# One full norm for two token tiles ahead of a 16-bit matrix product, in a two-layer decoder trunk

## The chip, the cores and the metric

The kernel runs on one NeuronCore of a Trainium2 chip. The metric is the time of one execution in device microseconds (us). Comparisons use the median of several runs. Engines are named as in the profile: PE is TensorE (matmuls; PEld its weight loads), DVE is VectorE, ACT is ScalarE, POOL is GpSimd, SP issues most of the transfers.

## What is computed

A trunk of two layers over 512 tokens of width 1024. Layer 0 has an attention mixer with two head groups (MoBA and NSA), layer 1 a forgetting attention (FoX). Each mixer is followed by a squared-ReLU MLP, and it is the two MLPs that the change touches. Cut to that part:

```python
def rmsnorm(x, g):
    xf = x.astype(jnp.float32)
    y = xf * lax.rsqrt(jnp.mean(xf * xf, axis=-1, keepdims=True) + RMS_EPS)
    return (y * g.astype(jnp.float32)).astype(x.dtype)

def sqrelu_mlp(h, w1, w2):
    a = jax.nn.relu(h @ w1)
    return (a * a) @ w2
...
for layer in range(DEPTH):
    hn = rmsnorm(h, mix_norm[layer])
    if layer % 2 == 0:
        h = h + moba_nsa_mixer(hn, ...)
    else:
        h = h + fox_mixer(hn, ...)
    h = h + sqrelu_mlp(rmsnorm(h, mlp_norm[layer]), mlp_w1[layer], mlp_w2[layer])
return rmsnorm(h, final_norm)
```

The hidden width of the MLP is 4096.

## The kernel before, in words

**Tiling.** The 512 tokens lie in four tiles of 128 (`hs[0]` to `hs[3]`, 128 partitions by 1024 columns). Matrix products get their accuracy from pairs: each operand is split into a high and a low part, and three matmuls (high by high, high by low, low by high; lines 135 to 137 in `mm3`) make one product.

**Banks.** PSUM has eight banks of 128 x 512 fp32 words. The program names them in four pairs, by tag: `s` (attention logits, later MLP results), `acc` (projections), `o` (attention outputs) and `pt` (transposes). `self.psum(tag)` takes a bank of the pair; it is free again when its last reader is through.

**Order of the work.** The program is written down in the order of `MIX0_ORDER` and `FOX_ORDER`, strings of steps. A planner then lays the instructions of every engine in a fixed order, by priorities and by a simulated timeline; so a change in one place can reorder work in another. In `MIX0_ORDER` the last steps are `m3 y o17 o6 o23`: the last pair of MoBA heads, step `y` (`prepare_rest`), and then three out-projections (`out_proj`, line 678 adds each result to `hs`) over head pairs 1 and 7, 6, and 2 and 3. In `FOX_ORDER` they are `p7 y o45 o67`. An out-projection runs over four token tiles and two halves of the columns, so eight bank-sized results, with three matmuls for each head pair in it. Its O tiles (the attention outputs, split in high and low) live in a pool of three buffers in layer 0.

**Step y.** The weights of the first MLP product are scaled into a 16-bit range by powers worked out from sums of squares. `scales16` adds up the sums over the partitions by a matmul with a matrix of ones (line 421), copies the result out of its bank (line 426) and makes the scale and its inverse on DVE (lines 427 to 429). In step `y` this is called with the tag `acc`; the matmul is tied to run behind `pv_last`, the last matmul of the attention so far, and the copy behind `v_last`, the last DVE step of the attention (in layer 0 the head sum of line 655). `up_split` then makes the 16-bit high and low weights (line 447 on ACT, 448 on DVE).

**The norm.** `norm_t16` handles the token tiles one by one. ACT squares the tile and sums it (line 388), DVE makes from this sum a rough factor `near` by bit operations on the number (lines 391 to 393), scales the tile by it and by the norm's weights in two halves (line 395), PE transposes eight blocks (line 400), ACT makes the 16-bit high part (line 403) and DVE the low part (line 404). As `near` is only near the true factor, a correction for each token is worked out afterwards (`row()`: full inverse root by `newton`, over `near`). `spread_row` turns it into a row along the free axis: four POOL products with the identity (line 195), a matmul with ones (line 196), a copy (line 197).

**The MLP.** It runs in eight steps of 512 hidden columns. `up(s)` makes four products of 128 hidden columns over all tokens; the product of `up(0)` is split in two halves of the tokens and held in four banks (two `acc`, two `s`). For every product ACT takes the relu and undoes the weights' scale (line 1189), POOL multiplies by the row (line 1190), and ACT squares (line 1192). `down(s)` multiplies with the second weight matrix by a Strassen scheme: `combos` makes sums of the activations (POOL, lines 1210 to 1215; splits on ACT, line 1200, and DVE, line 501), `weights` sums of the weights (line 1249 on DVE; splits on lines 1243 and 1244), PE runs line 1292, and DVE adds to `hs` (line 1300). The order of calls is `up(s + 1)` ahead of `down(s)`; the scales for `up(s + 2)` are made within `down(s)`.

Of the kernel before, what the change touches and what calls it, by code (L numbers as in the profile page):

```python
# [7 lines left out]
F32 = mybir.dt.float32  # L8
FR = mybir.dt.float32r
I32 = mybir.dt.int32  # L10
F16 = mybir.dt.float16
AF = mybir.ActivationFunctionType
ALU = mybir.AluOpType
AX = mybir.AxisListType

P = 128
S = 512
D = 1024
NT = S // P
# [5 lines left out]
RMS_EPS = 1e-5  # L25
ROOT_BITS = 0x5F3759DF
# [8 lines left out]
W_RAW = 1024  # L35
# [15 lines left out]
class Trunk:  # L51
# [133 lines left out]
            v.tensor_tensor(u, u, m, op=ALU.mult)  # L185
            v.scalar_tensor_tensor(y, u, -1.5, y, op0=ALU.add, op1=ALU.mult)

    def spread_row(self, y, sq_pool, pool):

        nc = self.nc  # L190
        diag = sq_pool.tile([P, S], F32, tag="r", name=self.nm("diag"))
        row = pool.tile([P, S], F32, name=self.nm("yrow"))
        ps = self.psum("pt")
        for t in range(NT):
            nc.gpsimd.tensor_scalar(diag[:, t * P:(t + 1) * P], self.ident, y[:, t:t + 1], 1.0, op0=ALU.mult, op1=ALU.mult)
        nc.tensor.matmul(ps, self.ones, diag, start=True, stop=True)
        nc.scalar.activation(row, ps, AF.Copy)
        return row

    def norm(self, h, dst, g):  # L200

        y = self.inv_rms(h, (0, D), lambda i: dst)
        for c in (slice(0, D // 2), slice(D // 2, D)):
            self.nc.vector.scalar_tensor_tensor(dst[:, c], h[:, c], y, g[:, c], op0=ALU.mult, op1=ALU.mult)
# [166 lines left out]
        self.bcast_row(g, row)  # L371
        return g

    def norm_t16(self, hs, g, gain, scratch, sq_pool, pool):

        nc = self.nc
        v = nc.vector
        x = self.xtp.tile([P, 2, KD, S], F16, tag="xhi", name=self.nm("x16"))  # L380
        ssq = pool.tile([P, NT + 1], F32, name=self.nm("ssq"))
        near, m, y, u = (pool.tile([P, NT], F32, name=self.nm("nr")) for _ in range(4))
        for t in range(NT):
            xn = self.raw.tile([P, W_RAW], F32, tag="raw", name=self.nm("xn"))
            one = lambda a: a[:, t:t + 1]
            halves = (slice(0, D // 2), slice(D // 2, D))
            for i, c in enumerate((slice(0, D),) if t < NT - 1 else halves):
                nc.scalar.activation(scratch[:, c], hs[t][:, c], AF.Square, accum_out=ssq[:, t + i:t + i + 1])
            if t == NT - 1:
                v.tensor_tensor(one(ssq), one(ssq), ssq[:, NT:], op=ALU.add)  # L390
            v.tensor_scalar(one(u).bitcast(I32), one(ssq).bitcast(I32), 1, None, op0=ALU.logical_shift_right)
            v.tensor_scalar(one(u).bitcast(I32), one(u).bitcast(I32), -1, ROOT_BITS, op0=ALU.mult, op1=ALU.add)
            v.tensor_tensor(one(near), one(u), gain, op=ALU.mult)
            for c in halves:
                v.scalar_tensor_tensor(xn[:, c], hs[t][:, c], one(near), g[:, c], op0=ALU.mult, op1=ALU.mult)
            for j in range(2):
                pt = self.psum("pt")
                for i in range(4):
                    k = 4 * j + i
                    nc.tensor.transpose(pt[:, i * P:(i + 1) * P], xn[:, k * P:(k + 1) * P], self.ident)  # L400
                pv = pt.rearrange("p (k c) -> p k c", k=4)
                dh, dl = (x[:, i, 4 * j:4 * j + 4, t * P:(t + 1) * P] for i in range(2))
                self.x_act = nc.scalar.activation(dh, pv, AF.Copy)
                self.x_dve = v.tensor_tensor(dl, pv, dh, op=ALU.subtract)  # L404

        def row():
            v.tensor_scalar(m, ssq[:, :NT], 0.5 / D, 0.5 * RMS_EPS, op0=ALU.mult, op1=ALU.add)
            self.newton(m, y, u)
            v.reciprocal(near, near)
            v.tensor_tensor(y, y, near, op=ALU.mult)  # L410
            return self.spread_row(y, sq_pool, pool)
        return (x[:, 0], x[:, 1]), row

    def scales16(self, squares, out, tag, behind=None):

# [42 lines left out]
    def prepare_mlp(self, layer):  # L458

        nc = self.nc  # L460
        st = self.const.tile([P, 3, 5], F32, name=self.nm("upst"))
        g8 = self.const.tile([P, KD], F32, name=self.nm("g8"))
        nc.sync.dma_start(g8, self.I["mlp_norm"][layer].rearrange("(p k) -> p k", k=KD))
        tiles = self.up_tiles(0)
        raws = self.up_load(layer, 0, self.raw, "raw", lambda f: tiles[f][:, 1], st[:, 0])
        nc.scalar.activation(g8, g8, AF.Square, accum_out=st[:, 0, 4:5])

        def rest():
            self.scales16(st[:, 0], st[:, 1:], "acc", self.pv_last)(self.v_last)
            self.first_up = self.up_split(raws, st[:, 1:], tiles), st[:, 1:]  # L470
        self.prepare_rest = rest

# [658 lines left out]
    def mlp(self, layer, hs, final=None):  # L1131
# [4 lines left out]
        nc, I = self.nc, self.I  # L1136
        w1, w2 = I["mlp_w1"][layer], I["mlp_w2"][layer]
        with ExitStack() as cx:
            pool = lambda name, bufs: cx.enter_context(self.tc.tile_pool(name=f"{name}{layer}", bufs=bufs))
            m3 = pool("mlpr", 3)  # L1140
            ma = pool("mlpa", 3)
            mt = pool("mlpt", 1)
            mg = pool("mlpg", 1)
# [5 lines left out]
            scratch = mg.tile([P, W_RAW], F16, name=self.nm("scratch"))  # L1149
            up_sq = [mg.tile([P, 4], F32, name=self.nm("upsq")) for _ in range(2)]  # L1150
            ready = {0: self.first_up}
            load = lambda s, pool, tag, *behind: self.up_load(layer, s, pool, tag, lambda f: scratch, up_sq[s % 2], *behind)

            def up_scale(s, tag, behind=None):
                sc = mg.tile([P, 2, 4], F32, name=self.nm("upsc"))
                return sc, self.scales16(up_sq[s % 2], sc, tag, behind)

            x, norm_row = self.norm_t16(hs, self.row_tile(I["mlp_norm"][layer], "g"), ready[0][1][:, 0, 4:5], scratch, m3, mg)
            after = self.x_act, self.x_dve
            raws1 = load(1, mr, "w", self.x_act)  # L1160
            row = norm_row()
            gf = None
            if final is not None:
                gf = mg.tile([P, D], F32, name="gf")
# [2 lines left out]
            def up(s):  # L1167

                act = [ma.tile([P, 2, 2, S // 2], F32, tag="act", name=self.nm("act")) for _ in range(2)]
                early = {}  # L1170
                w, undo = ready.pop(s)
                if s == 0:
                    tags = ("acc", "acc", "s", "s")
                    early = {f: self.psum(tags[f]) for f in range(nf)}
                    for part in ((0, 256), (256, 512)):
                        for f in range(nf):
                            self.proj_t(early[f], w[f], 0, x, part=part)
                            if part[0] and f == 0:
                                sc, step = up_scale(1, "o", self.mm_last)
                                step(self.x_dve)  # L1180
                                ready[1] = self.up_split(raws1, sc, self.up_tiles(1)), sc
                for f in range(4):
                    if f in early:
                        ps = early[f]
                    else:
                        ps = self.psum("acc")
                        self.proj_t(ps, w[f], 0, x)
                    r = m3.tile([P, S], F32, tag="r", name=self.nm("r"))
                    nc.scalar.activation(r, ps, AF.Relu, scale=undo[:, 1, f:f + 1])  # L1189
                    nc.gpsimd.tensor_tensor(r, r, row, op=ALU.mult)  # L1190
                    rv = r.rearrange("p (l c) -> p l c", l=2)
                    done = nc.scalar.activation(act[f // 2][:, :, f % 2], rv, AF.Square)  # L1192
                    if f == 1:
                        self.up_act = done
                return act
# [129 lines left out]
            def down_plain(s, act):  # L1325
# [3 lines left out]
                for t in range(NT):  # L1329
# [218 lines left out]
```

## Time and profile before

| | us |
|---|---|
| runs of the kernel (median of three) | 1260.73 (1259.74 to 1260.77) |
| the profiled execution, its own time | 1262.58 |
| its span in the trace | 1260.9 |
| DVE busy in the span | 930.6 |
| POOL busy in the span | 465.7 |
| MLP of layer 0, rough stretch | 326 to 640 |
| MLP of layer 1, rough stretch | 911 to 1233 |

In the profile, a row of the timeline gives the start, the length, the engine, the line of the program, the operation, the output and inputs by their names, and how many instructions were merged. `[0.78 <-DVE x L678]` at the end says that the engine had been idle for 0.78 us and that the end of a DVE instruction of line 678, on tile `x`, released it. The list of waits gives a total in us, how often it happened and the longest. The token tiles `hs` are called `x` in the profile, the first MLP weights `w` with scales `upst` (step 0) or `upsc`, the small norm tiles `nr`.

### The profile page before, as it was taken

Reading aid. Unit: us, or ns where it says so; the run is one execution under the profiler, and the core shown is the slowest. Engines: PE = TensorE matmul, PEld = TensorE weight load, DVE = VectorE, ACT = ScalarE, POOL = GpSimd, SP = SyncE. Lnnn points to the kernel's source line nnn. Section 1 sums busy time; section 2 is a strip of 40 time slices with the busy share of each in tenths; the row PEclk is TensorE's granted clock in tenths of the full one; section 3 lists DMA queues with packets and bytes.
Section 4 is the critical chain, followed back from the end, with each engine's and each line's share of the span. In section 5 each row is a group of like instructions: output and inputs, shape, how many; then the busy total and the mean of one; then the engine's idle time right before and its main releaser. Section 6 shows DMA issues by size and latency. Waiting matters only on the chain. (4 is left out here: it accounts for less than half of the span.)

```text
span 1260.9 us, 17472 instructions
## 1 busy us (share of the span) xinstructions
PE 1200.6 (95%) x6207; PEld 874.3 (69%) x6207; DVE 930.6 (74%) x1733; ACT 738.5 (59%) x1357; POOL 465.7 (37%) x469
## 2 busy tenths in 40 slices
PE   9999999997999999999998999999899999999997
PEld 7889987774856655566587887887675556655666
DVE  6877778676669767967876687576857787769775
ACT  7447656762565655565434785676467556655542
POOL 3435366543052252323301453444034332342324
PEclk9999999998999999999999999999999999999999
DMA  8952242231324333441303565546631344134301
GB/s 238 339 156 61 77 118 64 64 104 34 84 67 117 97 87 101 117 120 53 105 26 89 133 145 125 138 108 130 194 112 57 100 128 117 51 100 119 115 1 68
DMA packets 183731, 134.30 MB, mean 107 GB/s; under 512 B 48163, under 2 KB 158923, under 8 KB 183644
## 3 DMA queue, kind: packets, MB, share of 16 engines
q1 hardware_dynamic: 183484, 132.95, 37.4%
q8 instruction: 49, 0.80, 0.3%
q14 instruction: 38, 0.31, 0.1%
q10 hardware_dynamic: 160, 0.23, 0.0%
HBM read 120.28 MB, written 7.64 MB: 101 GB/s over the span
## 5 line engine op out<-in xcount | busy, mean ns | idle before, releaser
L1190 POOL TENSOR_TENSOR r<-r,yrow 128x512 f32<-128x512 f32 x64 | 119.9, 1876 | 315.3 <-ACT r L1189 315.3
L135 PE MATMUL acc<-x,w 128*128 128x512 f16 (+1 forms) x512 | 188.2, 368 | 4.7 <-ACT r L1189 4.0
L137 PE MATMUL acc<-x,w 128*128 128x512 f16 (+1 forms) x512 | 186.1, 368 | 3.4 <-DVE w L448 3.4
L136 PE MATMUL acc<-x,w 128*128 128x512 f16 (+1 forms) x512 | 188.0, 367 | 0.6 <-DVE x L404 0.6
L1292 PE MATMUL s<-whl,sp 128*128 128x512 f32 x672 | 180.3, 405 | 6.0 <-DVE x L1300 5.7
L1244 DVE TENSOR_TENSOR whl<-w,whl 128x1024 fp32r<-128x1024 f32 x98 | 124.6, 1281 | 78.6 <-ACT whl L1243 78.6
L1292 PEld LDWEIGHTS s<-whl,sp 128*128 128x128 f32 x672 | 124.9, 188 | 39.6 <-issue 7.0
L1243 ACT ACTIVATE whl<-w 128x1024 fp32r<-128x1024 f32 x98 | 102.5, 1052 | 40.2 <-PE o L1292 18.0
L93 ACT ACTIVATE whl<-raw 128x1024 fp32r<-128x1024 f32 (+1 forms) x75 | 77.5, 1043 | 67.7 <-PE acc L137 49.6
L1300 DVE TENSOR_TENSOR x<-s,x 128x512 f32<-128x512 f32 x112 | 76.0, 679 | 50.5 <-PE s L1292 50.5
L137 PEld LDWEIGHTS <-w 128*128 128x128 f16 x576 | 56.4, 98 | 63.0 <-issue 7.0
L135 PEld LDWEIGHTS <-w 128*128 128x128 f16 x576 | 56.4, 98 | 57.4 <-issue 7.1
L135 PE MATMUL acc<-xhi,whl 128*128 128x512 f32 x240 | 94.9, 396 | 1.1 <-DVE Q L503 0.8
L137 PE MATMUL acc<-xhi,whl 128*128 128x512 f32 x240 | 94.6, 394 | 1.3 <-POOL whl L100 0.8
L136 PEld LDWEIGHTS <-w 128*128 128x128 f16 x576 | 56.6, 98 | 56.4 <-issue 7.1
L1192 ACT ACTIVATE act<-r 128x512 f32<-128x512 f32 x64 | 40.0, 628 | 95.0 <-POOL r L1190 95.0
L136 PE MATMUL acc<-xlo,whl 128*128 128x512 f32 x240 | 94.0, 392 | 0.0
L100 POOL TENSOR_TENSOR whl<-raw,whl 128x1024 fp32r<-128x1024 f32 x27 | 67.1, 2486 | 67.6 <-ACT whl L93 66.9
L1292 PE MATMUL o<-whl,sp 128*128 128x512 f32 x336 | 87.7, 395 | 3.3 <-DVE whl L1244 3.3
L1189 ACT ACTIVATE r<-acc,upsc 128x512 f32<-128x512 f32 x56 | 38.0, 679 | 77.5 <-PE acc L137 76.9
L1249 DVE TENSOR_TENSOR w<-w,w 128x1024 f32<-128x1024 f32 x56 | 82.0, 1464 | 0.2
L1292 PEld LDWEIGHTS o<-whl,sp 128*128 128x128 f32 x336 | 62.1, 188 | 21.2 <-DVE whl L1244 5.9
(342 smaller groups left out, 2986.9 us busy)
## 6 DMA issues: line engine op xcount, KB each, us to landing
w<-in_mlp_w SPq DMA_DIRECT2D x120, 512.0 KB
raw<-in_odd_w_in SPq DMA_DIRECT2D x22, 512.0 KB
raw<-in_even_w_in SPq DMA_DIRECT2D x20, 512.0 KB
band<-bias_dram SPq DMA_DIRECT2D x24, 256.0 KB
bias_dram<-bias_rows SPq DMA_DIRECT2D x16, 320.0 KB
raw<-in_even_w_out SPq DMA_DIRECT2D x8, 512.0 KB
raw<-in_mlp_w SPq DMA_DIRECT2D x8, 512.0 KB
raw<-in_odd_w_out SPq DMA_DIRECT2D x8, 512.0 KB
```

Source lines behind the costliest of these rows:

```text
L93: nc.scalar.activation(hl[:, 0, :n], raw[:, :n], AF.Copy)
L100: eng.tensor_tensor(hl[:, 1, :n], raw[:, :n], hl[:, 0, :n].bitcast(F32), op=ALU.subtract)
L135: mm(ps, ahl[0], bhl[0], start=first, stop=False)
L136: mm(ps, ahl[0], bhl[1], start=False, stop=False)
L137: self.mm_last = mm(ps, ahl[1], bhl[0], start=False, stop=last)
L1190: nc.gpsimd.tensor_tensor(r, r, row, op=ALU.mult)
L1192: done = nc.scalar.activation(act[f // 2][:, :, f % 2], rv, AF.Square)
L1243: nc.scalar.activation(t[:, 0], src, AF.Copy)
L1244: nc.vector.tensor_tensor(t[:, 1], src, t[:, 0].bitcast(F32), op=ALU.subtract)
L1249: nc.vector.tensor_tensor(out, a_, b_, op=op)
L1292: mm = lambda l, r, first, last: nc.tensor.matmul(ps, l, r, start=first, stop=last, skip_group_check=True)
L1300: added = nc.vector.tensor_tensor(hv, ps, hv, op=ALU.add)
```

## The change

Four things change, all around the first MLP product:

1. The norm of a token tile uses the full inverse root. The squares of two tiles are summed, then one chain of small DVE operations works on both columns (mean and epsilon, `newton` with 11 operations, a product with the scaling gain and 1/32), and then both tiles are scaled and transposed. This is done for tiles 0 and 1 and again for tiles 2 and 3.
2. The row of correction factors is gone: `spread_row` with its POOL products, matmul and copy, and the small operations of `row()`.
3. The POOL product with the row between relu and square is gone. The factor that undoes gain and 1/32 is the same for all tokens and is given to the square as its `scale`; it is multiplied by 32 once in `rest()`.
4. In step `y` the sums for the scales go to a bank of tag `s` instead of `acc`.

```diff
@@ norm_t16
-        for t in range(NT):
-            xn = self.raw.tile([P, W_RAW], F32, tag="raw", name=self.nm("xn"))
-            one = lambda a: a[:, t:t + 1]
...
-            v.tensor_scalar(one(u).bitcast(I32), one(ssq).bitcast(I32), 1, None, op0=ALU.logical_shift_right)
-            v.tensor_scalar(one(u).bitcast(I32), one(u).bitcast(I32), -1, ROOT_BITS, op0=ALU.mult, op1=ALU.add)
-            v.tensor_tensor(one(near), one(u), gain, op=ALU.mult)
-            for c in halves:
-                v.scalar_tensor_tensor(xn[:, c], hs[t][:, c], one(near), g[:, c], op0=ALU.mult, op1=ALU.mult)
...
-        def row():
-            v.tensor_scalar(m, ssq[:, :NT], 0.5 / D, 0.5 * RMS_EPS, op0=ALU.mult, op1=ALU.add)
-            self.newton(m, y, u)
-            v.reciprocal(near, near)
-            v.tensor_tensor(y, y, near, op=ALU.mult)
-            return self.spread_row(y, sq_pool, pool)
-        return (x[:, 0], x[:, 1]), row
+        for t0 in range(0, NT, 2):
+            for t in (t0, t0 + 1):
+                for i, c in enumerate((slice(0, D),) if t < NT - 1 else halves):
+                    nc.scalar.activation(scratch[:, c], hs[t][:, c], AF.Square, accum_out=ssq[:, t + i:t + i + 1])
+            if t0:
+                v.tensor_tensor(ssq[:, NT - 1:NT], ssq[:, NT - 1:NT], ssq[:, NT:], op=ALU.add)
+            two = slice(t0, t0 + 2)
+            v.tensor_scalar(m[:, two], ssq[:, two], 0.5 / D, 0.5 * RMS_EPS, op0=ALU.mult, op1=ALU.add)
+            self.newton(m[:, two], y[:, two], u[:, two])
+            v.tensor_scalar(y[:, two], y[:, two], gain, 1 / 32, op0=ALU.mult, op1=ALU.mult)
+            for t in (t0, t0 + 1):
+                xn = self.raw.tile([P, W_RAW], F32, tag="raw", name=self.nm("xn"))
+                for c in halves:
+                    v.scalar_tensor_tensor(xn[:, c], hs[t][:, c], y[:, t:t + 1], g[:, c], op0=ALU.mult, op1=ALU.mult)
...
@@ prepare_mlp, rest()
-            self.scales16(st[:, 0], st[:, 1:], "acc", self.pv_last)(self.v_last)
+            self.scales16(st[:, 0], st[:, 1:], "s", self.pv_last)(self.v_last)
+            nc.vector.tensor_scalar(st[:, 2, 4:5], st[:, 2, 4:5], 32.0, None, op0=ALU.mult)
@@ mlp
-            x, norm_row = self.norm_t16(hs, self.row_tile(I["mlp_norm"][layer], "g"), ready[0][1][:, 0, 4:5], scratch, m3, mg)
+            gain = ready[0][1][:, :, 4:5]
+            x = self.norm_t16(hs, self.row_tile(I["mlp_norm"][layer], "g"), gain[:, 0], scratch, mg)
...
-            row = norm_row()
...
                     nc.scalar.activation(r, ps, AF.Relu, scale=undo[:, 1, f:f + 1])
-                    nc.gpsimd.tensor_tensor(r, r, row, op=ALU.mult)
                     rv = r.rearrange("p (l c) -> p l c", l=2)
-                    done = nc.scalar.activation(act[f // 2][:, :, f % 2], rv, AF.Square)
+                    done = nc.scalar.activation(act[f // 2][:, :, f % 2], rv, AF.Square, scale=gain[:, 1])
```

The transposes, the 16-bit split and the matmuls themselves are as before.

More of the change, by code (lines that the diff above doesn't have):

```diff
@@ L186, in newton @@
             v.scalar_tensor_tensor(y, u, -1.5, y, op0=ALU.add, op1=ALU.mult)
[L188 to L193, printed above, removed]
-        for t in range(NT):
[L195 to L198, printed above, removed]
     def norm(self, h, dst, g):
@@ L372, in row_tile, with norm_t16 @@
         return g
-    def norm_t16(self, hs, g, gain, scratch, sq_pool, pool):
+    def norm_t16(self, hs, g, gain, scratch, pool):
         nc = self.nc
@@ L381, in norm_t16 @@
         ssq = pool.tile([P, NT + 1], F32, name=self.nm("ssq"))
-        near, m, y, u = (pool.tile([P, NT], F32, name=self.nm("nr")) for _ in range(4))
-        for t in range(NT):
-            xn = self.raw.tile([P, W_RAW], F32, tag="raw", name=self.nm("xn"))
-            one = lambda a: a[:, t:t + 1]
[L386 to L390, printed above, removed]
-            v.tensor_scalar(one(u).bitcast(I32), one(ssq).bitcast(I32), 1, None, op0=ALU.logical_shift_right)
-            v.tensor_scalar(one(u).bitcast(I32), one(u).bitcast(I32), -1, ROOT_BITS, op0=ALU.mult, op1=ALU.add)
-            v.tensor_tensor(one(near), one(u), gain, op=ALU.mult)
-            for c in halves:
[L395 to L404, printed above, removed]
@@ L406, in row @@
-        def row():
-            v.tensor_scalar(m, ssq[:, :NT], 0.5 / D, 0.5 * RMS_EPS, op0=ALU.mult, op1=ALU.add)
-            self.newton(m, y, u)
-            v.reciprocal(near, near)
-            v.tensor_tensor(y, y, near, op=ALU.mult)
-            return self.spread_row(y, sq_pool, pool)
-        return (x[:, 0], x[:, 1]), row
+        m, y, u = (pool.tile([P, NT], F32, name=self.nm("nr")) for _ in range(3))
+        halves = (slice(0, D // 2), slice(D // 2, D))
+        for t0 in range(0, NT, 2):
[12 more added lines that the diff above has]
+                    v.scalar_tensor_tensor(xn[:, c], hs[t][:, c], y[:, t:t + 1], g[:, c], op0=ALU.mult, op1=ALU.mult)
+                for j in range(2):
+                    pt = self.psum("pt")
+                    for i in range(4):
+                        k = 4 * j + i
+                        nc.tensor.transpose(pt[:, i * P:(i + 1) * P], xn[:, k * P:(k + 1) * P], self.ident)
+                    pv = pt.rearrange("p (k c) -> p k c", k=4)
+                    dh, dl = (x[:, i, 4 * j:4 * j + 4, t * P:(t + 1) * P] for i in range(2))
+                    self.x_act = nc.scalar.activation(dh, pv, AF.Copy)
+                    self.x_dve = v.tensor_tensor(dl, pv, dh, op=ALU.subtract)
@@ L414, in scales16 @@
+        return x[:, 0], x[:, 1]
     def scales16(self, squares, out, tag, behind=None):
```

## The prediction

> **What bounds the kernel now.** I read the page's first part, then the waits of PE over the whole span, then tables by stretches of time, and then the timelines of the two places where layer 0 and layer 1 pass from the out-projection into the MLP. The page, and the longest waits of PE (total us, times, longest):
>
> ```profile
> span 1260.9 us, 17472 instructions
> PE 1200.6 (95%) x6207; PEld 874.3 (69%) x6207; DVE 930.6 (74%) x1733; ACT 738.5 (59%) x1357; POOL 465.7 (37%) x469
> ```
>
> ```profile
> PE acc L135 <- DVE x L678: 14.2, 18, 1.3
> PE s L1292 <- DVE x L1300: 5.7, 5, 1.4
> PE acc L135 <- ACT r L1189: 4.0, 2, 2.0
> PE acc L137 <- DVE w L448: 3.4, 6, 0.6
> PE o L1292 <- DVE whl L1244: 3.3, 7, 0.5
> ```
>
> TensorE is busy for 95% of the span, so work taken off POOL, DVE or ACT pays only where PE waits for it. The waits that this change can reach are these five; the first is the largest of the kernel. The next view gives two stretches (start:end, length, busy time of PE, PEld, DVE, ACT, POOL, clock, DMA): the second out-projection of layer 0, and a middle step of the MLP.
>
> ```profile
> 278.00:297.00 19.00, 13.52 (x52) 8.63 (x51) 4.84 (x7) 0.60 (x1) 0.55 (x1) 1.00 0.01 4
> 956.00:998.00 42.00, 42.00 (x185) 24.98 (x183) 33.90 (x41) 27.11 (x40) 14.44 (x10) 0.96 0.37 101
> ```
>
> In the MLP step PE has no idle time at all. In the out-projection it idles 5.48 us of 19, with DVE, ACT, POOL and the DMA all nearly idle too: nobody is overloaded, something is missing. The timeline shows what (start us, us):
>
> ```profile
> 278.12 0.28 PE L421 MATMUL acc<-upst,ones 128*128 128x5 f32 x2
> 280.69 0.50 PE L135 MATMUL acc<-whl,O 128*128 128x512 f32 x1 [0.78 <-DVE x L678]
> 295.40 0.50 PE L135 MATMUL acc<-whl,O 128*128 128x512 f32 x1 [0.78 <-DVE x L678]
> 297.84 0.50 PE L135 MATMUL acc<-whl,O 128*128 128x512 f32 x1 [0.78 <-DVE x L678]
> 318.83 0.40 PE L135 MATMUL acc<-whl,O 128*128 128x512 f32 x1
> 320.23 0.40 PE L135 MATMUL acc<-whl,O 128*128 128x512 f32 x1
> ...
> 282.40 0.69 DVE L678 TENSOR_TENSOR x<-acc,x 128x512 f32<-128x512 f32 x1 [1.76 <-PE acc L137]
> 300.89 0.16 DVE L426 COPY upst<-acc 128x5 f32<-128x5 f32 x1
> ```
>
> At 278.12 the scales' sums (L421) take one of the two acc banks, and the copy that empties it (L426) comes at 300.89. For 22.8 us the out-projection has one bank: it fills it, waits for the DVE add (L678), fills it again. A tile of six matmuls comes every 2.45 us (280.69 to 295.40 are six tiles); with two banks it comes every 1.40 (320.23 less 318.83, same shape, same line).
>
> **The change part by part.**
>
> *The bank.* The copy cannot come sooner by itself: it is tied to run behind the last DVE step of the attention, and that step waits for the out-projection, as the next rows show. POOL's rounding into an O tile waits for the projection's last matmuls, ACT's half of the head sum waits for POOL, DVE's half (L655) follows, then the copy.
>
> ```profile
> 296.45 0.62 POOL L507 TENSOR_SCALAR O<-o 128x512 fp32r<-128x512 f32 x1 [23.58 <-PE acc L137]
> 298.46 1.21 ACT L654 ACTIVATE o<-o 64x512 f32<-64x512 f32 x2 [1.01 <-POOL O L663]
> 299.46 1.40 DVE L655 TENSOR_TENSOR o<-o,o 64x512 f32<-64x512 f32 x2
> 303.05 4.27 ACT L447 ACTIVATE w<-w,upst 128x1024 f16<-128x1024 f32 x4 [3.39 <-DVE upst L428]
> 307.23 1.04 ACT L93 ACTIVATE whl<-raw 128x1024 fp32r<-128x1024 f32 x1
> 308.35 3.36 POOL L100 TENSOR_TENSOR whl<-raw,whl 128x1024 fp32r<-128x1024 f32 x1 [5.35 <-ACT whl L93]
> 311.76 0.79 PE L136 MATMUL acc<-whl,O 128*128 128x512 f32 x1
> ```
>
> With the sums in a logits bank both acc banks are free. The chain hangs on the last of the eight tiles, the one of 295.40, seven periods after the first. Each period is shorter by 1.05 us (2.45 less 1.40), so that tile comes 7.35 us sooner. What is late next is the chain quoted: O tile, head sum, copy, four weight conversions on ACT, the conversion of the last out-projection weights (L93, L100), and PE at 311.76. All of it is released by the projection's end, the load of those weights too, which waits for a raw buffer freed in the same chain. So it moves along whole. It may gain some more: the single-pair tiles from 297.84 on also start with one bank, and POOL's L100 (3.36) shares its time with DVE. Or it may lose: if the weights' load, not the chain, sets 307.23. I take -7.4, bounds -10 and -4. The logits bank itself costs nothing: the attention's last use of it lies before 278, its next user is the first MLP product at about 327, and the copy frees it near 293. In layer 1 I count nothing for the bank; its sums were copied out quickly there.
>
> *The norm.* Per layer the counts on DVE hardly change: away go 12 one-column and 14 four-column operations, in come 26 two-column ones and one times 32. What changes is when. Now a token tile is scaled as soon as its own squares are summed; afterwards tiles 0 and 1 both wait for tile 1's sum and then for a chain of 13 dependent small operations. The rows of layer 0:
>
> ```profile
> 321.91 0.18 ACT L388 ACTIVATION_READ_ACCUMULATOR scratch<-x 128x1 f32 x1
> 322.96 0.69 DVE L678 TENSOR_TENSOR x<-acc,x 128x512 f32<-128x512 f32 x1 [0.30 <-PE acc L137]
> 324.17 1.41 DVE L395 SCALAR_TENSOR_TENSOR xn<-x,nr,g 128x512 f32<-128x512 f32 x2
> 334.50 0.16 DVE L184 TENSOR_TENSOR nr<-nr 128x4 f32<-128x4 f32 x1
> 334.69 0.16 DVE L185 TENSOR_TENSOR nr<-nr,nr 128x4 f32<-128x4 f32 x1
> 336.83 1.46 DVE L404 TENSOR_TENSOR x<-pt,x 128x512 f16<-128x512 f32 x2 [1.58 <-ACT x L403]
> ...
> 326.00 1.03 PE L400 MATMUL pt<-ident,xn 128*128 128x128 f32 x8
> 327.28 0.27 PE L135 MATMUL acc<-x,w 128*128 128x256 f16 x1 [0.25 <-ACT x L403]
> 339.60 1.02 PE L196 MATMUL pt<-diag,ones 128*128 128x512 f32 x2
> 340.46 0.27 PE L135 MATMUL s<-x,w 128*128 128x256 f16 x1
> 340.79 0.27 PE L135 MATMUL acc<-x,w 128*128 128x256 f16 x1
> ```
>
> Tile 1's sum is there at 322.09. Thirteen steps at 0.19 us (334.69 less 334.50) are 2.5, and one add of the out-projection (0.6) falls between: 325.2. Tile 1's first half is the third scaled half, 0.7 us each (1.41 for two): 327.3. From the first transposes to the first matmul took 1.28 us (326.00 to 327.28): 328.6, against 327.28, so +1.3. The low parts (L404, 0.7 each) queue on DVE behind the scaling, some 0.3 more. I take +1.6 per layer, bounds +0.9 (no add between, low parts hidden) and +3.0 (a second add and two low parts in front); below nothing is excluded, since tile 1's sum comes no sooner. Queued behind the chain on DVE are the out-projection's last adds, which free acc banks, but PE is then past its last tile. Tiles 2 and 3 have a cover: their low parts end at 338.29 and the second half of the tokens begins in acc at 340.79. The chain there puts 14 dependent steps, 2.7 us, in the place of a few; that fits into those 2.5 us and the start's own delay of 1.6. Without that cover it would cost up to 2.
>
> *The row of factors.* Its matmul on PE goes: 339.60 to 340.46, 0.86 us per layer, and PE is dense there, so -1.7 in all. Its four POOL products and one ACT copy per layer lie off the path.
>
> *The row products.* POOL loses 64 of these, and ACT's square follows ACT's relu directly:
>
> ```profile
> L1190 POOL TENSOR_TENSOR r<-r,yrow 128x512 f32<-128x512 f32 x64 | 119.9, 1876 | 315.3 <-ACT r L1189 315.3
> ```
>
> ```profile
> 954.92 0.38 PE L135 MATMUL acc<-x,w 128*128 128x512 f16 x1 [2.02 <-ACT r L1189]
> 942.93 2.29 DVE L1249 TENSOR_TENSOR w<-w,w 128x1024 f32<-128x1024 f32 x1
> 950.23 1.21 DVE L1249 TENSOR_TENSOR w<-w,w 128x1024 f32<-128x1024 f32 x1
> ```
>
> The 120 us of POOL time are not on PE's path in the middle steps (the 42.00 above). They are once per layer: the last product of up(1) waits 2.02 us for a bank, because ACT's relu stands behind conversions of combinations that POOL makes late, one of its products before each. Without three products of 1.3 us or more in front, the combinations come about 4 us earlier, and they leave the DVE stretch in which L1249 takes 2.29 us instead of 1.21. I take the wait as gone, -2.0 per layer, -4.0 in all; bounds 0 (ACT's order stays bad) and -5.7 with the clock, below.
>
> *The middle steps.* The other three waits sum to 12.4 us (5.7, 3.4, 3.3) and all end in DVE, which POOL slows where they meet. Most meetings in those bursts are with the combinations, which stay. I take -1.5, bounds -5 and +3: the program's order is planned anew, and the combinations move.
>
> *The clock.* The table of stretches, for the 4 us after layer 1's wait:
>
> ```profile
> 954.00:958.00 4.00, 3.08 (x10) 1.17 (x10) 4.00 (x5) 2.29 (x4) 1.76 (x2) 0.71 0.36 98
> ```
>
> After a PE gap of 2.02 us the granted clock fell to 0.71 over these 4 us, worth some 1.2 us. The same gap in layer 0 cost no clock, and the sum counts nothing for it. So at the two new gaps in front of the MLP (about 2 us each, where there was one of 0.25) the row would charge up to 2.4 in all, and the sum below would be -9.0 instead of -11.4.
>
> [...]
>
> **Sum.** -7.4 (bank) +3.2 (norm) -1.7 (row) -4.0 (wait in up(1)) -1.5 (middle steps) = -11.4. The profiled execution took 1262.58 (span 1260.9 and 1.7 around it), 1.85 above the median of the runs, 1260.73. So 1251.2 for it, and 1249.3 for the median; I give 1249.
>
> **The rivals.**
>
> *The second bank brings nothing* because the last weights, not the chain, set the start of the last out-projection. For it: L93 at 307.23 is a conversion of freshly loaded weights. Against: it starts as the fourth L447 ends (303.05 and 4.27). Then the 7.4 are lost to a new wait of PE in front of L136: 1256.7. Chance 0.10.
>
> *The pair's chain costs its upper bound and the clock.* A gap of 3 us in front of each MLP, and 1.2 us at a low clock behind each: +5.2 over the forecast, 1254.5. For it: the row of 0.71. Against: in layer 0 no clock was lost. Chance 0.14.
>
> *Slower.* The combinations, no longer held back by row products, move into the DVE bursts of the down products, where each meeting stretches a DVE operation by 1.1 us (2.29 against 1.21). Place: the 14 steps that combine. One more meeting on PE's path per step is +15.4, less the forecast's 11.4: +4.0 or 1264.7. It decides from about 1.0 us per step on (11.4 and 2.5 over 14 steps). Against: PE has no idle time in the whole step shown, so the first part of it is absorbed. Chance 0.05.
>
> **How the numbers follow.** Forecast 0.71. Its terms at their bounds, added as roots of squares, are +3.4, +2.8, +4.0 and +4.5 on the slow side, 7.4 together, and -2.6, -1.4, -1.7 and -3.5 on the fast side, 4.9 together: 1244 to 1256.5. A difference under 0.2% (2.5 us) could not be told from none. Faster than 1258.2: the forecast, most of the first rival, nearly all of the second: 0.89. Within 0.2%: 0.06. Slower: 0.05. The range for 8 in 10 takes these bounds, half a microsecond more on the fast side for the clock that layer 1 may win back, and with them the second rival and nearly the first: 1243.5 to 1256.5.
>
> **What would show it.** Right: out-projection tiles every 1.4 us from 278 on in layer 0, and the MLP of layer 0 beginning some 6 us sooner; waits on L678 down from 14.2 to about 8; PE's gap before the first MLP matmul about 2 us in both layers; no wait on L1189; POOL about 120 us less busy. Wrong: gaps of 0.78 that remain after 278, or a new wait of PE for POOL's L100 of several us, or waits on L1300 and L1244 that grow.

## The result and the profile after

The changed kernel takes 1252.18 us (median of four runs, 1250.99 to 1254.8), the kernel before 1260.75 beside it: ratio 0.9934, 95% interval 0.9915 to 0.9953. That is 8.6 us less, where 11.7 were forecast (1249 against 1260.73). The profiled execution took 1250.99. Its page begins:

```profile
span 1249.3 us, 17383 instructions
...
PE 1195.4 (96%) x6203; PEld 875.8 (70%) x6203; DVE 925.7 (74%) x1735; ACT 746.7 (60%) x1355; POOL 343.7 (28%) x397
```

The span is 11.6 us shorter, and POOL does 122 us less. The waits of PE (total, times, longest), where L661, L1172 and L1274 are the lines that were L678, L1189 and L1292, and L389 is a transpose of the norm:

```profile
PE acc L135 <- DVE x L661: 7.3, 9, 1.3
PE pt L389 <- DVE xn L384: 4.9, 2, 2.5
PE o L1274 <- DVE whl L1226: 4.5, 10, 0.6
PE pt L389 <- DVE x L393: 2.3, 2, 1.3
PE acc L136 <- POOL whl L100: 2.0, 1, 2.0
...
PE acc L135 <- ACT r L1172: 0.6, 1, 0.6
```

The wait for the out-projection's adds is halved (14.2 before) and the stall of 4.0 in `up(1)` is down to 0.6. New are 7.2 us in front of the norm's transposes (4.9 and 2.3), and the wait for the splits of the second weights (L1226, which was L1244) grew from 3.3 to 4.5. The timeline of layer 0 shows the bank's part:

```profile
271.71 0.45 PE L135 MATMUL acc<-whl,O 128*128 128x512 f32 x1
...
286.09 0.28 PE L403 MATMUL s<-upst,ones 128*128 128x5 f32 x2
...
287.99 0.17 DVE L408 COPY upst<-s 128x5 f32<-128x5 f32 x1
...
310.87 0.40 PE L137 MATMUL acc<-whl,O 128*128 128x512 f32 x1
```

Out-projection tiles now run from about 270 on, among the attention's last matmuls, and the last matmul comes at 310.87. Before it was this row:

```profile
325.76 0.39 PE L137 MATMUL acc<-whl,O 128*128 128x512 f32 x1
```

Then comes the norm's part, DVE's and PE's rows together:

```profile
307.44 0.19 ACT L374 ACTIVATION_READ_ACCUMULATOR scratch<-x 128x1 f32 x1
307.71 0.16 DVE L378 TENSOR_SCALAR nr<-ssq 128x2 f32<-128x2 f32 x1
...
308.50 0.69 DVE L661 TENSOR_TENSOR x<-acc,x 128x512 f32<-128x512 f32 x1 [0.23 <-PE acc L137]
...
309.90 0.69 DVE L661 TENSOR_TENSOR x<-acc,x 128x512 f32<-128x512 f32 x1 [0.25 <-PE acc L137]
...
311.30 0.69 DVE L661 TENSOR_TENSOR x<-acc,x 128x512 f32<-128x512 f32 x1 [0.25 <-PE acc L137]
...
312.49 0.23 DVE L380 TENSOR_SCALAR nr<-nr,upst 128x2 f32<-128x2 f32 x1
...
312.87 2.74 DVE L384 SCALAR_TENSOR_TENSOR xn<-x,nr,g 128x512 f32<-128x512 f32 x4
313.77 1.60 PE L389 MATMUL pt<-ident,xn 128*128 128x128 f32 x8 [2.50 <-DVE xn L384]
...
316.33 1.97 PE L389 MATMUL pt<-ident,xn 128*128 128x128 f32 x8 [0.97 <-DVE x L393]
...
318.13 0.59 PE L135 MATMUL acc<-x,w 128*128 128x256 f16 x2
```

The chain of thirteen runs from 307.71 to 312.72. It is 5.0 us long because three adds of the out-projection stand within it in DVE's order (308.50, 309.90 and 311.30, 0.69 each), each waiting some 0.24 us for PE. Four scalings follow in one go, the second tile's transposes wait for a bank, and the first product starts 7.26 us after the last out-projection matmul; before it was 1.52 (325.76 to 327.28). Layer 1 shows the same (7.10). The products then run at half clock (0.50 to 0.53), as the column after POOL's busy time shows (start:end, length, busy time of PE, PEld, DVE, ACT, POOL, granted clock):

```profile
312.80:314.50 1.70, 0.70 (x5) 0.52 (x6) 1.70 (x4) 0.07 (x1) 0.00 (x0) 1.00 0.00 0
314.50:316.20 1.70, 0.86 (x4) 0.46 (x4) 1.70 (x5) 1.13 (x2) 0.00 (x0) 0.53 0.00 0
...
319.60:321.30 1.70, 1.70 (x10) 1.20 (x9) 1.56 (x7) 0.00 (x0) 0.00 (x0) 0.50 0.77 217
321.30:323.00 1.70, 1.70 (x16) 1.52 (x15) 1.70 (x3) 0.00 (x0) 0.00 (x0) 0.96 0.30 86
```

From marks read off the two timelines, the difference of the spans divides as follows (after less before, us).

| stretch | difference |
|---|---|
| to the last out-projection matmul, layer 0 | -14.9 |
| from there to the first MLP product, both layers | +5.7, +5.6 |
| from there to the end of `up(1)`, both layers | -0.9, -4.7 |
| from there to the end of `up(7)`, both layers | -3.3, -1.8 |
| last down products of layer 0 | +0.4 |
| from there to the last out-projection matmul of layer 1 (its attention) | +1.7 |
| after `up(7)` of layer 1 | +0.5 |
| sum (before rounding) | -11.6 |

### The profile page after: what moved, and what is told of

Same layout as the page of the kernel before. It is cut to its first block, busy times and chain, and to the rows that moved or that the text cites. A ratio compares the mean times of both kernels' runs of the same rounds, so it can differ in the third digit from the quotient of the medians.

```text
span 1249.3 us, 17383 instructions
## 1 busy us (share of the span) xinstructions
PE 1195.4 (96%) x6203; PEld 875.8 (70%) x6203; DVE 925.7 (74%) x1735; ACT 746.7 (60%) x1355; POOL 343.7 (28%) x397
## 5 line engine op out<-in xcount | busy, mean ns | idle before, releaser
L1274 PE MATMUL s<-whl,sp 128*128 128x512 f32 x672 | 178.5, 404 | 1.6 <-DVE x L1282 1.6
L1274 PEld LDWEIGHTS s<-whl,sp 128*128 128x128 f32 x672 | 125.2, 188 | 31.9 <-DVE x L1282 2.4
L484 DVE TENSOR_TENSOR sp<-act,sp 128x512 fp32r<-128x512 f32 x64 | 63.5, 1012 | 92.7 <-ACT sp L1182 92.6
L1226 DVE TENSOR_TENSOR whl<-w,whl 128x1024 fp32r<-128x1024 f32 x98 | 120.1, 1235 | 14.8 <-ACT whl L1225 14.8
L1172 ACT ACTIVATE r<-acc,upsc 128x512 f32<-128x512 f32 x56 | 38.2, 682 | 138.1 <-PE acc L137 138.0
L1192 POOL TENSOR_TENSOR t<-act 128x512 f32<-128x512 f32 x14 | 24.6, 1760 | 325.9 <-ACT act L1174 321.7
L1274 PE MATMUL o<-whl,sp 128*128 128x512 f32 x336 | 89.8, 399 | 7.0 <-DVE whl L1226 4.5
L100 POOL TENSOR_TENSOR whl<-raw,whl 128x1024 fp32r<-128x1024 f32 x27 | 66.9, 2477 | 69.7 <-ACT whl L93 69.0
L1274 PEld LDWEIGHTS o<-whl,sp 128*128 128x128 f32 x336 | 61.4, 188 | 28.6 <-DVE whl L1226 9.1
L1231 DVE TENSOR_TENSOR w<-w,w 128x1024 f32<-128x1024 f32 x56 | 72.2, 1289 | 10.7 <-issue 5.6
```

The lines of the kernel that those rows point to most:

```text
L100: eng.tensor_tensor(hl[:, 1, :n], raw[:, :n], hl[:, 0, :n].bitcast(F32), op=ALU.subtract)
L484: self.nc.vector.tensor_tensor(out, ps, hi.bitcast(F32), op=ALU.subtract)
L1226: nc.vector.tensor_tensor(t[:, 1], src, t[:, 0].bitcast(F32), op=ALU.subtract)
L1231: nc.vector.tensor_tensor(out, a_, b_, op=op)
L1274: mm = lambda l, r, first, last: nc.tensor.matmul(ps, l, r, start=first, stop=last, skip_group_check=True)
```

## The experiments

The theory after this result: the second bank carries the whole net gain; the full norm costs about what the removed row brings; and part of the norm's price is half clock. The rivals: norm and row bring half of the gain; or the order of DVE's queue, not the chain, makes the gap. Every ratio is to the kernel before on the same chip.

| kernel | median us | ratio, 95% interval | span | mean clock |
|---|---|---|---|---|
| changed kernel, first | 1252.18 | 0.9934 (0.9915 to 0.9953) | 1249.3 | 0.987 |
| changed kernel, again | 1251.59 | 0.9931 (0.9916 to 0.9946) | 1250.5 | 0.986 |
| bank only | 1249.31 | 0.9898 (0.9881 to 0.9915) | 1247.6 | 0.990 |
| all but the bank | 1264.09 | 1.0009 (0.9998 to 1.0021) | 1261.1 | 0.989 |
| row product back | 1266.94 | 1.0041 (1.0029 to 1.0053) | 1263.2 | 0.982 |
| rough factor | 1240.70 | 0.9827 (0.9811 to 0.9843) | 1239.4 | 0.992 |
| single tiles | 1247.82 | 0.9884 (0.9865 to 0.9903) | 1246.3 | 0.991 |
| single tiles, again | 1248.34 | 0.9900 (0.9876 to 0.9924) | 1248.7 | 0.988 |
| unread products | 1252.24 | 0.9931 (0.9918 to 0.9944) | 1248.8 | 0.989 |
| four transpose banks | 1250.50 | 0.9920 (0.9906 to 0.9934) | 1249.2 | 0.987 |
| single, four banks, order | 1250.81 | 0.9910 (0.9895 to 0.9925) | 1249.1 | 0.985 |
| the same, unread products | 1248.26 | 0.9896 (0.9878 to 0.9913) | 1246.5 | 0.991 |
| single, unread products | 1247.54 | 0.9883 (0.9861 to 0.9906) | 1245.2 | 0.992 |

**The bank alone.** One word of the kernel before is changed:

```diff
-            self.scales16(st[:, 0], st[:, 1:], "acc", self.pv_last)(self.v_last)
+            self.scales16(st[:, 0], st[:, 1:], "s", self.pv_last)(self.v_last)
```

> The kernel before with one word changed: the scales' sums lie in a logits bank; norm, row and products stay as before. Theory (the bank carries the whole net gain, the rest of the change about cancels): the last out-projection matmul of layer 0 comes at about 311 instead of 325.8 as in the changed kernel, the gap to the first product stays near 1.5, some of the 14.9 us is given back on the way, and the time is about 1249 (1246 to 1251), no slower than the whole change. Rival (norm and row bring half of it): 1254 to 1257. Second rival (the bank brings nothing by itself): 1259 to 1261.

Measured 0.9898. Its timeline at the end of layer 0's out-projection (the norm is the one of before, with L400 as its transpose):

```profile
312.10 0.40 PE L137 MATMUL acc<-whl,O 128*128 128x512 f32 x1
312.34 1.04 PE L400 MATMUL pt<-ident,xn 128*128 128x128 f32 x8
...
313.63 0.27 PE L135 MATMUL acc<-x,w 128*128 128x256 f16 x1 [0.25 <-ACT x L403]
```

The out-projection ends 13.7 us sooner than before, the gap stays 1.5, and the time is below that of the whole change. Its interval ends at 0.9915, those of the changed kernel's two sets begin at 0.9915 and 0.9916. By these ratios, which come from different chips, one word is worth some 0.3 per cent more than the four changes together.

**Everything but the bank.** The changed kernel with that word put back.

> The changed kernel with the scales' sums put back into an out-projection bank. Theory (bank carries the net gain): out-projection ends near 325.8 again, norm's gap of about 7 stays, its two prices of 5.7 and 5.6 are about paid by the row that is gone, and the time is 1259 to 1263, about that of the kernel before. Rival (norm and row bring half): 1255 to 1257. If the stall of the first bank covers the norm chain, so that both prices were counted twice, it is 1254 to 1256 too, but with a gap of under 4 in front of the first product.

Measured 1.0009 (0.9998 to 1.0021): no measurable difference from before; the median of 1264.09 lies 1.1 us above the forecast. The first product starts at 330.03, 7.3 us after the last out-projection matmul. That matmul comes at 322.76, 3.0 us sooner than before and not near 325.8 as expected. The gaps of 0.78 are all there again, but between 256 and 322.8 the clock is full, where the kernel before ran 10.2 us at half clock. Both runs together show the first theory: the bank carries the net gain, and norm and row cancel or lose a little.

**The row product put back.** The changed kernel with POOL's product between relu and square, by a row that holds ones:

```diff
+            row = mg.tile([P, S], F32, name=self.nm("yrow"))
+            nc.gpsimd.memset(row, 1.0)
...
                     nc.scalar.activation(r, ps, AF.Relu, scale=undo[:, 1, f:f + 1])
+                    nc.gpsimd.tensor_tensor(r, r, row, op=ALU.mult)
```

> The changed kernel with GpSimd's product put back between the two ScalarE operations of each strip, by a row that holds ones. Theory (the row's product is what held the bank at the step without banks to spare, and what made the middle steps longer): the wait of 4.0 us on the first ScalarE operation in the second step is back, the seven middle steps of a layer are longer by 2 to 3 us, and the time is 1258 to 1264, so that the kernel without the bank's change would be slower than before. Rival (GpSimd's product is hidden and the gain there came with another order): 1252 to 1254.

Measured 1.0041, against 0.9931 on the same chip: some 14 to 15 us more, above the forecast's upper end. The waits:

```profile
PE s L1277 <- DVE x L1285: 7.6, 5, 1.9
...
PE acc L137 <- DVE w L430: 3.5, 6, 0.6
PE acc L135 <- ACT r L1174: 2.8, 2, 2.0
```

The stall in `up(1)` is back in part (2.8 of 4.0), with the waits of the kernel before on the adds of the down products and the weights' split. From the end of `up(1)` to that of `up(7)` it takes 3.7 us longer in layer 0 and 8.8 in layer 1 than in the changed kernel's second profile, where 2 to 3 were forecast. The mean clock is 0.982, so up to 22.7 us of the span are lost to it (1263.2 by 0.018) against 16.2 in the changed kernel. So the product is not hidden, though POOL is no busier than the 37% of the span that it had before the change.

**The rough factor.** In place of the chain, three operations for each single tile, as in the kernel before, and no correction behind them; so this kernel leaves out the exact norm:

```diff
-        for t0 in range(0, NT, 2):
+        for t in range(NT):
...
-            self.newton(m[:, two], y[:, two], u[:, two])
...
+            v.tensor_scalar(one(u).bitcast(I32), one(ssq).bitcast(I32), 1, None, op0=ALU.logical_shift_right)
+            v.tensor_scalar(one(u).bitcast(I32), one(u).bitcast(I32), -1, ROOT_BITS, op0=ALU.mult, op1=ALU.add)
+            v.tensor_tensor(one(y), one(u), gain, op=ALU.mult)
```

> The changed kernel with only the rough factor for each tile (three VectorE operations instead of thirteen for two tiles, one tile at a time), and nothing that corrects it: it leaves out the Newton steps, and with them the exactness of the norm. Theory (the gap of 7 in front of the first product is the chain and its pairing): gap about 2, the price of 5.7 and 5.6 falls to under 1.5 each, time 1241 to 1244. Rival (the gap is the order of VectorE's queue and the two transpose banks, not the chain): gap still over 4, 1247 to 1251.

Measured 0.9827, 1240.70 us, just below the range. The gap in front of the first product is 1.5 us in both layers, as before the change:

```profile
311.85 0.40 PE L137 MATMUL acc<-whl,O 128*128 128x512 f32 x1
312.09 1.04 PE L387 MATMUL pt<-ident,xn 128*128 128x128 f32 x8
313.37 0.27 PE L135 MATMUL acc<-x,w 128*128 128x256 f16 x1 [0.25 <-ACT x L390]
```

The gap is the chain and its pairing, then. Four kernels with the second bank now make a square (their kernels before differ by 2 us between chips, so the sums are good to about that): rough factor with row 1249.3, rough without row 1240.7, full with row 1266.9, full without row 1251.6. The row costs 8.6 us under the rough factor and 15.3 under the full norm; the full norm costs 10.9 without the row and 17.6 with it. (The full norm with a row is the one with ones, which has the product but not the making of the row.) The change takes the price of the norm to save that of the row: 1249.3 to 1251.6.

**Single tiles.** The full norm, but one chain for each tile:

```diff
-        for t0 in range(0, NT, 2):
+        for t in range(NT):
...
-            self.newton(m[:, two], y[:, two], u[:, two])
+            self.newton(one(m), one(y), one(u))
```

> The changed kernel with the full norm for one token tile at a time in place of two: the thirteen small VectorE operations run four times per layer instead of twice, but the first tile's can begin when its own squares are there (about 4.7 us sooner). Theory (the pair's wait for its second tile and the lump of four scalings make up a part of the gap of 7): first product about 1.5 us sooner per layer, 1248 to 1251. Rival (26 more small operations on VectorE cost as much as they bring, since the out-projection's additions stand between them): 1252 to 1254.

Measured 0.9884, 1247.82 us, just below the forecast. The gap is 6.2 and 6.7 us (316.30 less 310.08, 902.02 less 895.33): only 1.0 and 0.4 less than in the changed kernel. Tile 0's transposes come early, but PE then waits 3.09 us for tile 1. Its span is 3.0 us shorter than the changed kernel's, and its mean clock of 0.991 for 0.987 alone is worth up to 5.0 (1246.3 by 0.009 against 1249.3 by 0.013), so in this pair of profiles the rest of the kernel does not get faster. I ran it again:

> The norm by single token tiles once more, on one chip with the next kernel. If its 0.5 per cent below the whole change are its own, 1246 to 1249 and five to six stretches at half clock again; if they came by chance of the clock, more stretches and 1249 to 1252.

0.9900, the median within 1246 to 1249, but with a clock of 0.988 and eight steps of half clock (a step is 3.4 us at 0.50 and costs up to 1.7) where the first had five. The medians of both sets lie below the changed kernel's, the second interval overlaps with its; how much of the difference is the clock's stays open.

**The changed kernel again**, for the same question:

> The changed kernel once more, beside the kernel before on the same chip as the three that follow. If the stretches at half clock (two of 6.8 us and one of 3.4 in the attention, two more in front of the products) hang on the program, its profile shows them at the same places and its time is 1251 to 1253. If they fall by chance, the profile shows another number of them and the time moves in steps of about 1.7.

Neither holds whole. The time is the same and the steps of half clock are nine in both profiles, but at other places: in the first, half clock in front of layer 1's product lasted 3.4 us, in the second 6.8; in the attention of layer 1 one stretch of the first was 6.8 us where the second has 3.4. The places go with the execution, not with the program alone.

**Products that nobody reads.** Behind the last out-projection matmul, in the changed kernel:

```diff
+        with self.tc.issue_after(self.mm_last.ins):
+            idle = self.psum("o")
+            for _ in range(3):
+                nc.tensor.matmul(idle, self.ones, hs[2][:, D // 2:], start=True, stop=True)
```

> The changed kernel with three products more on TensorE that nobody reads, issued behind the last out-projection matmul of each layer, so that TensorE works through the wait for the normed tile. Theory (that wait of 2.5 us, with the single transposes behind it, is what halves the clock for 6.8 us in layer 0 and 3.4 us in layer 1 at the first products): these two stretches are gone, the first product starts at the same time or up to 0.5 us later, and the time is 1246 to 1250. Rival (the clock falls because of the transposes, or the three products push them back): the stretches stay, 1252 to 1255.

```profile
310.74 2.74 PE L373 MATMUL o<-x,ones 128*128 128x512 f32 x6
313.32 1.38 PE L393 MATMUL pt<-ident,xn 128*128 128x128 f32 x8
...
315.97 1.25 PE L393 MATMUL pt<-ident,xn 128*128 128x128 f32 x8 [1.27 <-DVE x L397]
317.31 0.38 PE L135 MATMUL acc<-x,w 128*128 128x256 f16 x2
```

```profile
311.10:323.00 11.90, 10.32 (x72) 7.34 (x71) 11.01 (x31) 3.11 (x6) 0.00 (x0) 1.00 0.31 90
```

The first row, six instructions, is the three products. The mechanism is as the theory has it: with PE busy through the wait, the clock is full (1.00) from 311 to 323, and in layer 1 (1.00) from 901 to 911. The last matmul of `up(1)` in layer 0 starts 2.9 us sooner (362.08 against 364.99). Yet the time is 0.9931, as without it. Some 2.0 us of the lead are left at the end of layer 0's `up(7)`, 1.5 at the first out-projection matmul of layer 1 (753.18 against 754.67), and none when the out-projection ends (899.47 against 899.42). The attention's timeline has this row:

```profile
875.95 0.41 PE L623 MATMUL o<-HT,v 128*64 128x512 f16 x2 [2.98 <-DMA HT<-HL]
```

PE waits 2.98 us for a transfer where it was 1.2, and a step of half clock follows from 876.5 to 879.9 (a clock of 0.67 over 875.5 to 880.6). This place took what was left of the lead.

**Four transpose banks.** In the changed kernel:

```diff
-                    pt = self.psum("pt")
+                    pt = self.psum(("pt", "o")[j])
```

> The changed kernel with the transposes of a token tile in two kinds of banks, so that those of a pair have four instead of two. Theory (the second eight wait 0.97 us and 1.34 us for a bank): these waits go, the first product comes 0.7 to 1.3 us sooner per layer, 1249 to 1252. Rival (they then wait for the third and fourth scaling, which end hardly sooner, or for the copies out of the banks): 1251.5 to 1253.

The gap is 5.85 and 5.76 us, 1.4 and 1.3 less, so the bank's wait is gone, as the theory said. The time, 0.9920 (0.9906 to 0.9934), cannot be told from 0.9931. Here too the wait for the transfer in layer 1 is 3.0.

**All together.** Single tiles, four transpose banks, and the chains of tiles 2 and 3 behind tile 1's scaling:

```diff
+            with self.tc.issue_after(scaled.ins) if t > 1 else ExitStack():
...
+                self.newton(one(m), one(y), one(u))
...
```

> The kernel with the norm for one tile at a time, with four transpose banks in place of two and the chains of the third and fourth tile put behind the second tile's scaling on VectorE. Theory (of the 3.09 us that TensorE waits for the second tile with the norm by single tiles, about 1 us is small operations of the later tiles that stand in between): that wait falls to about 2 us in each layer, and the time is 1244 to 1248, below both kernels. Rival (what the single tiles brought lies in fewer stretches at half clock, not in the wait): the wait is shorter but the time stays within 1246.5 to 1250.

A miss: PE's wait for tile 1 is 3.00 and 2.90, and the time of 1250.81 lies above both ranges. What stands between tile 0's scaling and tile 1's on DVE are the last add (0.68) and tile 0's two low parts (0.69 and 0.68), not small operations alone.

> The same with three products on TensorE that nobody reads, behind the first tile's transposes, so that TensorE works while it waits for the second tile. Theory (the waits in front of the first products halve the clock for at least 3.4 us a layer): no stretch at half clock there in either layer, 1.7 us less per layer, 1242 to 1246. Rival (the three products push the second tile's transposes back, or what is won is lost at the later wait for a DMA transpose in layer 1, as with the three products in the changed kernel): 1246 to 1250.

Three unread products behind tile 0's transposes bring 1248.26. No half clock lies in front of the products in either layer (1.00 from 306.0 to 663.0 and from 878.9 to 1242), yet the rival's range holds: the wait for the transfer in layer 1 is 2.1. The last kernel has single tiles, two banks, and the unread products in an `s` bank:

> The norm by single token tiles, two transpose banks as in the changed kernel, and three unread products on TensorE, in a logits bank, behind the first tile's transposes. Theory (the bank of the attention's results that the four kernels with unread products or four transpose banks used is what made the wait for a DMA transpose in layer 1 grow from 1.3 to 2.1 or 3.0 us): that wait is 1.3 again, the stretches at half clock in front of the products are gone, 1243 to 1246. Rival (that wait follows from the time at which layer 1 begins, or the clock's stretches only move to another place): 1246 to 1249.

```profile
310.56 0.39 PE L137 MATMUL acc<-whl,O 128*128 128x512 f32 x1
...
311.08 1.29 PE L387 MATMUL pt<-ident,xn 128*128 128x128 f32 x8
312.21 2.74 PE L396 MATMUL s<-x,ones 128*128 128x512 f32 x6
315.46 1.29 PE L387 MATMUL pt<-ident,xn 128*128 128x128 f32 x8 [0.51 <-DVE xn L382]
316.77 0.38 PE L135 MATMUL acc<-x,w 128*128 128x256 f16 x2
```

PE's wait for tile 1 falls from 3.09 to 0.51 idle, the clock stays full (1.00 from 304.3 to 661.3 and from 877.2 to 1241), but the wait for the transfer is 2.2 without the `o` bank. The time, 1247.54, is the rival's. The theory on that bank falls; why the wait differs between these kernels stays open. At 0.9883 (0.9861 to 0.9906) this is, with the plain single tiles, the lowest of those that compute the full result, and below both kernels: the changed kernel's intervals begin at 0.9915. From the bank alone, 0.9898 (0.9881 to 0.9915), it cannot be told apart.

## Why the prediction came out right

The time lies in the range and the forecast is 3 us low, but the terms were not right one by one. Two large errors cancelled, and that was luck.

- *Bank: -7.4 forecast, -14.9 found (-13.7 alone), outside the bounds.* The mechanism was right; the size was not. The sum counted seven periods, from 280.69 to the tile of 295.40, and let all that follows move along unchanged. The stretch from the first to the last out-projection matmul, of before and then of after:

```profile
181.30:325.80 144.50, 127.06 (x629) 98.82 (x628) 107.72 (x294) 83.60 (x199) 65.86 (x82) 0.94 0.22 64
```

```profile
181.20:310.90 129.70, 118.69 (x621) 96.22 (x619) 105.44 (x293) 82.80 (x198) 65.76 (x82) 0.97 0.25 70
```

  PE's idle time went from 17.4 to 11.0 us: from 255 on, the waits on the adds fall from 13 with 10.1 us to 5 with 3.7. A period was 1.05 us longer with one bank although the gap shows as 0.78, so each gap costs another 0.27 that counts as busy; eight gaps fewer are about 2.2 (an estimate). The eight transposes of tile 0, within the stretch before, stand behind it after, some 0.9. Two steps at half clock remain of five, 5.1 us less. Together these are 14.6 of the 14.9, but the last part need not be the bank's. One of the three steps lies at 249 to 256, ahead of the stall, and the kernel with everything but the bank has the same stall and no half clock from 256 to the end of its out-projection. In the runs, though, the bank alone brings 12.9 us (0.9898 of 1262.45) at the same mean clock (0.990 against a median of 0.989). How much of the clock's share belongs to the bank stays open. The forecast's doubt about POOL's L100 was sound, but small: a wait of 2.0. For layer 1 nothing was counted, and with the bank alone its attention takes as long as before, 145.4 us from the first to the last out-projection matmul against 145.3.
- *Norm: +3.2 forecast, +11.3 found, far above the upper bound of 6.0.* I put one add into the chain; there were three, and each had to wait for PE. I took the start of tile 1's transposes from its first scaled half; their banks were not free, because the low parts that free them (L393) stand behind all four scalings. Of the 4.1 us by which the gap of 7.26 exceeds the forecast's 3.1, some 2 are the longer chain (5.0 for 3.1) and some 1.4 the wait for banks. And the first products ran at half clock, which costs some 1.6 more behind them in layer 0 (318.13 to 321.3 at 0.50). The step that failed is the one that took DVE's order of the kernel before for that of the changed one.
- *Row's matmul and the wait in `up(1)`: -5.7 forecast, -0.9 and -4.7 found.* Right in sum. Half clock behind the new gap reaches into this stretch in both layers; in layer 1 the step behind the old stall (the prediction's row of 0.71) goes in return. That the product by the row had a part in the wait is shown by putting it back: 2.8 us of 4.0 return. It is not the only cause: without the product the same wait is 2.0 with everything but the bank, 2.0 and 1.8 with single tiles and 2.0 with four transpose banks, 0.6 in the changed kernel. The order of the work on ACT, which the forecast named for its bound of 0, may have the rest; no run here shows it.
- *Middle steps: -1.5 forecast, -5.1 found, just outside the bound of -5.* From `up(2)` to `up(7)` each step takes 41.35 us instead of 42.29, 4.7 less per layer; the second step gives 1.4 and 3.0 back. In layer 0 the waits on the down products' adds and on the first weights' split fall from 4.4 us to 1.2 over these steps. I read "no idle time of PE" from one stretch that began at half clock; the step from 447 to 489 has 1.37 us of idle PE (40.63 busy of 42). Under the rough factor the row as a whole costs 8.6 us, not far from the 7.2 of the forecast's three terms (1.7, 4.0 and 1.5); under the full norm it costs 15.3, up to 6.5 of it by the clock.
- *Clock: nothing forecast.* In these profiles as much is lost to it over the span after as before (0.987 and 0.986 against 0.987): the stretches of 310.6 in the out-projection and of 955.7 in `up(1)` went, others came in front of the products (314.6 and 905.1) and grew in the attention of layer 1 (four steps in the first profile where before has two; the whole stretch is 1.7 us longer). But the profile of before was one with a low clock. In the runs of the second set, on one chip, the median clock is 0.991 before and 0.987 after, which is up to 5 us (1250 by 0.004) that the sum had at nothing. The low rows stand at 0.50, and the stretches of these profiles last 3.41 or 6.83 us and so cost some 1.7 or 3.4 (an estimate from their length and clock), at places that move between two executions of one program. In layer 0 of the changed kernel gaps of 2.50 and 0.97 with sparse transposes between them came ahead of the 6.8 us at 0.50 in front of the products, and in the kernel with the unread products, which filled the first, that stretch is gone (1.00 from 311 to 323).

Of the rivals, the second named the mechanism that did come, a longer chain and half clock behind it, with a gap of 3 us where 7 came; that the range held is the bank's doing, whose 7.5 us too many met the norm's 8.1. The slower rival did not come. Of the signs named ahead, the tiles every 1.4 us, the waits on L678 near 8 (7.3) and POOL's 120 us came as said. The MLP of layer 0 began 9.15 us sooner, not 6; 0.6 us of the wait on L1189 are left; the gap of about 2 us in front of the MLP was 7. Of the signs against it three came in part: four gaps of 0.68 to 0.92 in front of the single-pair tiles, the wait of 2.0 for L100, and the grown wait on L1244. The exchange of the row for the full norm brings nothing measurable here, and the bank alone gives 1249.3.

## What to carry to other kernels

A tiny result that sits in one bank of a pair until a late copy costs the whole pair (here a tile every 2.45 us instead of 1.40); look for evenly spaced short gaps and move it to a bank that nobody needs. Before a chain of small operations is put ahead of TensorE, read which large operations will stand within it on its engine in order: thirteen steps of 0.2 us, 2.5 in all, became 5.0. And when terms of a change can be built alone, time them alone: here one word brought at least as much as the whole.

## What the hardware showed beyond the forecast

In these profiles half clock comes in lengths of 3.4 or 6.8 us at 0.50, so up to 1.7 or 3.4 us lost each time, five to twelve steps of 3.4 us in a profile besides its last microseconds. The two profiles of the single tiles had five and eight, worth up to 5 us, and their spans differ by 2.4; the six runs of the changed kernel's second set reach from 1249.84 to 1256.82. Most of the differences between the last seven kernels of the table are smaller than that. And a wait of 2.98 us for a transfer, in the midst of dense matmuls, was itself followed by a step.

The same gap did not always cost the same. The kernel before has a gap of 2.02 us in `up(1)` of both layers (start:end, length, busy time of PE, PEld, DVE, ACT, POOL, granted clock):

```profile
368.60:372.01 3.41, 1.96 (x10) 0.89 (x10) 3.41 (x3) 1.71 (x4) 1.59 (x1) 1.00 0.11 12
952.26:955.67 3.41, 1.39 (x7) 0.67 (x6) 3.41 (x4) 2.52 (x5) 1.06 (x2) 1.00 0.00 0
955.67:959.08 3.41, 3.41 (x10) 1.22 (x8) 2.62 (x3) 2.48 (x4) 2.12 (x2) 0.50 0.52 154
```

In layer 0 the gap begins ahead of the first row and ends at 370.06; PE is busy for 57% of that row, and the clock stays at 1.00 in the 3.41 us behind it. In layer 1 the gap lies whole in its row, of which PE is busy for 41%, and the 3.41 us behind it are the step that the prediction's row of 0.71 shows. So the length of the gap alone does not decide it here: in one execution 2.02 us cost nothing at one place and a step at the other.
